# 128-row score matmuls, inverse root of the query and key norms on GpSimd, a split residual: a hybrid decoder layer on one core

## The chip, the cores and the metric

One core of a Trainium2 chip (trn2). The time is device microseconds for one execution of the whole program; the number given for a kernel is the median of its runs. Engines are named as in the profile: PE is TensorE's matmuls and PEld its weight loads, DVE is VectorE, ACT is ScalarE, POOL is GpSimd, SP is the queue that issues most of the DMAs.

## The reference

One step of a decoder layer with 1024 prompt tokens and 8 sequences of 4 sample tokens, model width 1024. Attention (4 heads, each a pair of 64-wide query and key halves) and an RG-LRU recurrence share the input and the output projection; a gated FFN with a width-3 convolution follows. What the change touches is the prompt's attention and the sum that follows it:

```python
q = partial_rope(rmsnorm(q.reshape(bsz, t_len, ATT_HEADS, 2, QK_SUB_DIM), p['g_q']), pos)
k = partial_rope(rmsnorm(k.reshape(bsz, t_len, ATT_HEADS, 2, QK_SUB_DIM), p['g_k']), pos)
...
s = jnp.einsum('bqhcd,bkhcd->bhcqk', q, k) * (QK_SUB_DIM ** -0.5)
s = jnp.where(mask, s, jnp.finfo(F32).min)
p = jax.nn.softmax(s, axis=-1)
p_diff = p[:, :, 0] - lam * p[:, :, 1]
o = jnp.einsum('bhqk,bkhd->bqhd', p_diff, v)
...
m = jnp.concatenate([attn_out, lru_out], axis=-1) @ p['w_out']
x = x + gt1 * m
```

## The kernel before

Nearly every product is made of three fp32r matmuls, high by high, low by high and high by low part of the two operands (`mm3`, L153 to L157). The program has five stages: norm, modulation and LRU with its projections (to about 190 us of the profiled execution), the value projection (190 to 235), prompt attention (245 to 517), output projection with sample attention and the second norm (517 to 690), and the FFN (690 to the end). The order of instructions on each engine is set by a scheduler that simulates the program on a timeline; each engine then runs its own queue in that order, and a transfer waits in SP's queue behind what stands ahead of it.

Prompt attention runs over 16 groups g = head h by pair of 128-row query blocks pr. Each group has these parts, interleaved with those of its neighbours:

- `qk_mm` projects queries and keys three groups ahead. `qk_norm` calls `sums` (ACT copies and squares, DVE reduces to 8 sums of squares per row) and `normed`: DVE L660 and the eleven instructions of `rsqrt_dve` (L136 to L142) give the inverse root on 128x8 elements, then POOL multiplies (L662, L666) and applies rope (L673 to L676, tile rp).
- `qk_T` transposes on PE and splits queries and keys into parts. QA holds for each c (0 and 1) 128 rows: the high part of one half of the query in the 64 rows of that c, and its low part in the other 64. KA holds the high part of the key twice, so that one 128-row matmul gives high by high and low by high. KL holds the low part of the key, the two halves c one above the other.
- `score(g, x, c)` for query block x of the pair and softmax c: per 256 keys one 128-row matmul of QA and KA (L744) and one matmul on the 64 rows `me` of QA and KL (L745); then a mask matmul (L746), the row maximum on DVE (L750) and the exponential with its row sum on ACT (L752). Its result lies in one of two PSUM banks.
- `combine` (L755 to L764) subtracts the two softmaxes, unnormalised, and writes the first sum times a constant into le, one DVE instruction per block (L764). `pv_T` transposes the result, `pv` multiplies by the values; its output goes through tile oT to DRAM.

The residual x2 (8 blocks m of 128 rows by 1056 columns) is allocated in `output`, after attention's pools are closed, and loaded there in four DMAs by `x2_load` (L1153 and L1156), the first for blocks 0 to 3 and columns 0 to 383. `accumulate` (L1080) adds the output projection to it; the first such sums (L1084) free the PSUM banks that sample attention then takes. In the LRU stage `softplus` works on 128x4 elements (7 DVE instructions, one of ACT, 19 of POOL); its input `lru_lambda` and its work tile sp_e lie in the pool lp.

Of the kernel before, what the change touches and what calls it, by code (L numbers as in the profile page):

```python
# [6 lines left out]
F32 = mybir.dt.float32  # L7
# [137 lines left out]
class Build:  # L145
# [56 lines left out]
    def front(self):  # L202
# [158 lines left out]
        lcs = self.load(lp, "state_lru_conv", [128, 4, NS, 3])  # L361
        lamb = self.load(lp, "lru_lambda", [128, 4])
        wgh = ada.tile([128, 2, 4, 128], F32R, name="wgh")
        wgl = ada.tile([128, 2, 4, 128], F32R, name="wgl")
        lco = lp.tile([128, 4, 27], F32, name="lco")
        lho = lp.tile([128, 4, 9], F32, name="lho")
# [177 lines left out]
        b = proj(3)  # L544
        evac(3, b)
        W.split_to(7)
        ada_next()
# [39 lines left out]
        self.pages = []  # L587
        vpp = pool("v", side="right")
        vp = vpp.__enter__()
        vh = [vp.tile([128, 8, 256], F32R, name=f"vh{b}") for b in range(2)]  # L590
        vl = [vp.tile([128, 8, 256], F32R, name=f"vl{b}") for b in range(2)]

# [36 lines left out]
        lpp.__exit__(None, None, None)  # L629
        SP.dma_start(a["lru_conv_o"], lco)  # L630
        SP.dma_start(a["lru_h_o"], lho)
# [12 lines left out]
        G.tensor_copy(mkb, mk)  # L644
        g64 = "p x (g d) -> p (x g) d"

        def sums(b, X, n, st):

            S.activation(st, b, AF.Copy)
            sq = stage("qk_sq")[:n, :X]  # L650
            S.activation(sq, b, AF.Square)
            ms = p.tile([128, 3, 8], F32, name="qk_ms", tag="qk_ms", bufs=2)
            ms = tuple(ms[:n, j, :4 * X] for j in range(3))
            V.tensor_reduce(ms[0], sq.rearrange(g64, d=64), axis=AX.X, op=ALU.add)
            return ms

        def normed(s, i0, X, n, st):

            ms, y, t = s
# [35 lines left out]
        def qk_T(g):  # L695
# [38 lines left out]
        def score(g, x, c):  # L734
            h, pr = divmod(g, 4)
            n = (2 * pr + x + 1) * 128
            b = sbank("s_ps")
            me = slice(64 * c, 64 * c + 64)
# [10 lines left out]
            l = EX[g, x, "l"]  # L749
            V.tensor_reduce(l[:, c:c + 1], b[:, :n], axis=AX.X, op=ALU.max, negate=True)  # L750
            e = EX[g, x, c] = p.tile([128, 1024], F32, name="p_e", tag=f"p_e{c}", bufs=4 if c == 0 else 2)
            S.activation(e[:, :n], b[:, :n], AF.Exp, bias=l[:, c:c + 1], accum_out=l[:, 2 + c:3 + c])  # L752

        def combine(g, x):


            h, pr = divmod(g, 4)
            i = 2 * pr + x
            n = (i + 1) * 128
            l, p0, p1 = EX.pop((g, x, "l")), EX.pop((g, x, 0)), EX.pop((g, x, 1))  # L760
            V.reciprocal(l[:, 3:4], l[:, 3:4])
            V.scalar_tensor_tensor(l[:, 3:4], l[:, 2:3], lam, l[:, 3:4], op0=ALU.mult, op1=ALU.mult)
# [18 lines left out]
        def pv(g, b):  # L781
# [35 lines left out]
        for g in range(NG):  # L817
# [81 lines left out]
        app.__exit__(None, None, None)  # L899
        vpp.__exit__(None, None, None)  # L900
        self.psb = psp

# [169 lines left out]
    def output(self):  # L1072
        a, V, S, G, PE, SP, W = self.a, self.V, self.S, self.G, self.PE, self.SP, self.W
        pool, act_at = self.pool, self.act_at
        xpp = pool("x2", side="right")
        x2 = xpp.__enter__().tile([128, NK, T], F32, name="x2")
        steps = Steps()
        env = {}

        def accumulate(b, m, i, gt, pl):  # L1080

            t0, tw = TC[i]
            w = min(tw, SEQ - t0)
            V.scalar_tensor_tensor(x2[:, m, t0:t0 + w], b[:, :w], gt[:, m, 0:1], x2[:, m, t0:t0 + w], op0=ALU.mult, op1=ALU.add)  # L1084
            if tw > w:
                t = pl.tile([128, SAMP], F32, name="acc_s", tag="acc_s", bufs=2)
                V.tensor_tensor(t.rearrange("p (s q) -> p s q", s=NS), b[:, w:tw].rearrange("p (s q) -> p s q", s=NS),
                                gt[:, m, 1:, None].to_broadcast([128, NS, DT]), op=ALU.mult)
                V.tensor_tensor(x2[:, m, SEQ:], t, x2[:, m, SEQ:], op=ALU.add)

        def norm2(i, env, acc):
# [15 lines left out]
            if tw > w:  # L1107
                ts = p.tile([128, NK, SAMP], F32, name="u2s", tag=tags[0], bufs=2)
                V.tensor_tensor(ts, x2[:, :, SEQ:], bc[:, None, w:tw].to_broadcast([128, NK, SAMP]), op=ALU.mult)
            ut = None  # L1110
            for k in range(NK + 1):
# [9 lines left out]
                V.scalar_tensor_tensor(t[:, :w], x2[:, k, t0:t0 + w], A[:, k, 0:1], bc[:, :w],  # L1121
                                       op0=ALU.mult, op1=ALU.mult)
# [11 lines left out]
        def squares(i, mg, p, tags, acc):  # L1134
            t0, tw = TC[i]
            for m in range(4 * mg, 4 * mg + 4):
                if acc is None:
                    acc = p.tile([128, 384], F32, name="n2_acc", tag=tags[0], bufs=2)
                    S.activation(acc[:, :tw], x2[:, m, t0:t0 + tw], AF.Square)
                else:  # L1140
                    q = p.tile([128, 384], F32, name="n2_sq", tag=tags[1], bufs=tags[2])
                    S.activation(q[:, :tw], x2[:, m, t0:t0 + tw], AF.Square)
                    (V if mg or i == 2 else G).tensor_tensor(acc[:, :tw], acc[:, :tw], q[:, :tw], op=ALU.add)
# [8 lines left out]

        def x2_load(m, n, t0, tw):  # L1153
            SP.dma_start(x2[:, m:m + n, t0:t0 + tw], a["xT"][m:m + n, :, t0:t0 + tw].rearrange("m p t -> p m t"))

        x2_load(0, 4, 0, 384)  # L1156
        for m in range(4):
# [6 lines left out]
        with pool("ps_c", space=PSUM) as pp:  # L1164
# [74 lines left out]

            V.tensor_copy(x2[:1, 4:, 0:1], gsubT[:1, None].to_broadcast([1, 4, 1]))  # L1240
            V.tensor_copy(x2[:1, :, 384:385], gsubT[:1, None].to_broadcast([1, NK, 1]))
# [29 lines left out]
        with pool("ffn") as p, pool("ps_d", space=PSUM) as pp:  # L1271
# [130 lines left out]
            def down(cs, last):  # L1402
# [4 lines left out]
                while todo:  # L1407
# [9 lines left out]
                    for b, (m, i) in zip(bs, batch):  # L1417
# [7 lines left out]
                        if last:  # L1425
                            SP.dma_start(a["yT"][m][:, t0:t0 + tw], x2[:, m, t0:t0 + tw])
                W.split_to(self.ffn_unit["d", cs[-1]] + 3)
# [11 lines left out]
            SP.dma_start(a["ffn_conv_o"], fo)  # L1439
        xpp.__exit__(None, None, None)  # L1440
        self.sqp.__exit__(None, None, None)
# [131 lines left out]
```

## Time and profile before

| | |
|---|---|
| runs | 1434.02, 1430.48, 1433.25 us; median 1433.25 |
| profiled execution | 1431.46 us |
| its span, first to last instruction | 1429.6 us |
| PE / PEld / DVE / ACT / POOL busy, share of the span | 97% / 91% / 57% / 39% / 30% |
| mean granted clock of PE, share of full speed | 0.978 |
| attention, 245 to 520 us: PE / PEld / DVE / ACT / POOL busy us of 275 | 268.0 / 224.9 / 184.7 / 146.3 / 91.5 |

A busy time says how long an engine had an instruction in work; PE's matmuls overlap, so how dense they are is seen from their starts, not from the busy share. PEld overlaps PE where the load of the next weights runs beside the matmul before. The granted clock is the share of TensorE's full speed that the chip let it run at: 1.00 is 2.4 GHz, 0.50 is 1.2 GHz.

### The profile page before, as it was taken

What the parts mean: (1) busy time and instruction counts of PE and PEld (TensorE: products, weight loads), DVE (VectorE), ACT (ScalarE), POOL (GpSimd) and SP (SyncE); (2) the same over time, 40 slices, a digit from 0 to 9 for tenths busy, and PEclk for the clock granted to TensorE, in tenths of its full rate; (3) what the DMA queues carried; (4) which work ended last, traced back from release to release, by engine and by line L of the source; (5) the groups of instructions that cost most, each with busy time, mean ns of one, the idle gap of its engine ahead of it and who ended that gap; (6) DMA issues with size and microseconds to landing.
All of it is one profiled execution on the core that took longest, in us unless ns stands there. A gap on an engine that the chain in (4) does not pass through costs nothing.

```text
span 1429.6 us, 23840 instructions
## 1 busy us (share of the span) xinstructions
PE 1380.3 (97%) x9520; PEld 1302.9 (91%) x9520; DVE 810.8 (57%) x1700; ACT 553.5 (39%) x981; POOL 427.3 (30%) x504
## 2 busy tenths in 40 slices
PE   3998999999999989999999999999999999999998
PEld 3898999788878777789999999999999999999998
DVE  5759534876667436578764545353545353635356
ACT  4366623554545532326723232314141414142411
POOL 1162114433334022413633232314141414142320
PEclk8999999998999899999999999999999999999999
DMA  8625351101011287502111010102020202020203
GB/s 337 253 91 182 144 186 56 50 16 45 20 42 58 70 299 245 187 29 72 45 45 60 30 60 31 60 30 60 30 70 20 75 16 75 15 74 17 73 16 133
DMA packets 51936, 121.99 MB, mean 85 GB/s; under 512 B 8274, under 2 KB 25554, under 8 KB 48754
## 3 DMA queue, kind: packets, MB, share of 16 engines
q1 hardware_dynamic: 46914, 115.73, 24.1%
q10 hardware_dynamic: 4912, 4.74, 1.0%
q8 instruction: 75, 1.23, 0.4%
q14 instruction: 35, 0.29, 0.1%
HBM read 106.51 MB, written 13.94 MB: 84 GB/s over the span
## 4 chain that ended last, share of the span: by engine, by line
PE 89%; DVE 6%; ACT 2%; DMA 2%; issue 1%; POOL 0%; SPq 0%; DVEq 0%; ACTq 0%; POOLq 0%
PE up L155 12%; PE up L156 12%; PE up L157 12%; PE dn L157 6%; PE dn L156 6%; PE dn L155 6%; PE s_ps L745 3%; PE qk_ps L155 3%; PE qk_ps L156 3%; PE qk_ps L157 3%; PE s_ps L744 2%; PE wo_ps L155 2%; PE wo_ps L157 2%; PE wo_ps L156 1%; PE qk_pt L774 1%
## 5 line engine op out<-in xcount | busy, mean ns | idle before, releaser
L60 POOL TENSOR_TENSOR w_lo<-w_raw,w_hi 128x1024 fp32r<-128x1024 f32 x90 | 223.7, 2494 | 592.4 <-ACT w_hi L59 500.9
L155 PE MATMUL up<-act_h,w_hi 128*128 128x384 f32 (+1 forms) x1056 | 341.4, 324 | 1.9 <-ACT act_h L1129 1.9
L157 PE MATMUL up<-act_h,w_lo 128*128 128x384 f32 (+1 forms) x1056 | 340.2, 323 | 0.8 <-DVE w_lo L60 0.8
L156 PE MATMUL up<-act_l,w_hi 128*128 128x384 f32 (+1 forms) x1056 | 340.8, 323 | 0.0
L1084 DVE SCALAR_TENSOR_TENSOR x<-dn,modT,x 128x384 f32<-128x384 f32 (+1 forms) x264 | 149.6, 570 | 167.9 <-PE dn L157 167.7
L1306 DVE SCALAR_TENSOR_TENSOR fy<-fx,conv_ffn_w,fy 128x1072 f32<-128x1072 f32 (+2 forms) x92 | 137.9, 1500 | 173.2 <-ACT fy L1304 171.9
L155 PEld LDWEIGHTS up<-act_h,w_hi 128*128 128x128 f32 x1056 | 197.9, 188 | 2.4 <-ACT act_h L1129 2.2
L157 PEld LDWEIGHTS up<-act_h,w_lo 128*128 128x128 f32 x1056 | 198.3, 188 | 1.1 <-DVE w_lo L60 1.1
L59 ACT ACTIVATE w_hi<-w_raw 128x1024 fp32r<-128x1024 f32 x94 | 98.0, 1057 | 261.7 <-PE dn L156 151.3
L156 PEld LDWEIGHTS up<-act_l,w_hi 128*128 128x128 f32 x1056 | 198.3, 188 | 0.0
L157 PE MATMUL dn<-hh,w_lo 128*128 128x384 f32 (+1 forms) x528 | 170.5, 323 | 0.0
L156 PE MATMUL dn<-hl,w_hi 128*128 128x384 f32 (+1 forms) x528 | 170.5, 323 | 0.0
L155 PE MATMUL dn<-hh,w_hi 128*128 128x384 f32 (+1 forms) x528 | 169.7, 321 | 0.0
L155 PEld LDWEIGHTS dn<-hh,w_hi 128*128 128x128 f32 x528 | 99.2, 188 | 0.0
L157 PEld LDWEIGHTS dn<-hh,w_lo 128*128 128x128 f32 x528 | 99.1, 188 | 0.0
L156 PEld LDWEIGHTS dn<-hl,w_hi 128*128 128x128 f32 x528 | 99.1, 188 | 0.0
L155 PE MATMUL qk_ps<-w_hi,act_h 128*128 128x256 f32 (+1 forms) x288 | 85.9, 298 | 0.0
L157 PE MATMUL qk_ps<-w_hi,act_l 128*128 128x256 f32 (+1 forms) x288 | 84.1, 292 | 0.0
L156 PE MATMUL qk_ps<-w_lo,act_h 128*128 128x256 f32 (+1 forms) x288 | 84.1, 292 | 0.0
L750 DVE TENSOR_REDUCE ls<-s_ps 128x1 f32<-128x128 f32 (+7 forms) x64 | 48.1, 755 | 54.1 <-PE s_ps L746 53.8
L155 PE MATMUL wo_ps<-act_h,w_hi 128*128 128x384 f32 (+1 forms) x192 | 62.7, 338 | 2.8 <-ACT p_e L752 1.1
L156 PE MATMUL wo_ps<-act_l,w_hi 128*128 128x384 f32 (+1 forms) x192 | 62.4, 326 | 0.0
(323 smaller groups left out, 2653.4 us busy)
## 6 DMA issues: line engine op xcount, KB each, us to landing
w_ada<-w_ada SPq DMA_DIRECT2D x24, 1024.0 KB, 6.3
w_raw<-w_up SPq DMA_DIRECT2D x44, 512.0 KB, 3.6
w_raw<-w_down SPq DMA_DIRECT2D x22, 512.0 KB, 3.5
w_raw<-w_in SPq DMA_DIRECT2D x20, 512.0 KB, 3.7
page<-cache_v SPq DMA_DIRECT2D x32, 256.0 KB, 5.0
xT<-xT SPq DMA_DIRECT2D x8, 528.0 KB, 7.9
w_raw<-w_out SPq DMA_DIRECT2D x8, 512.0 KB, 3.8
kp<-cache_k SPq DMA_DIRECT2D x16, 256.0 KB, 4.7
```

Of the source, the lines that this page charges most:

```text
L59: self.nc.scalar.activation(hi, self.raw[i], AF.Copy)
L60: (eng or self.nc.gpsimd).tensor_tensor(lo, self.raw[i], hi.bitcast(F32), op=ALU.subtract)
L155: self.PE.matmul(out, lh, rh, start=first, stop=False)
L156: self.PE.matmul(out, lh, rl, start=False, stop=False)
L157: self.PE.matmul(out, ll, rh, start=False, stop=last)
L744: PE.matmul(o, q, KA[4 * h + kp][:, c, :w], start=True, stop=False, skip_group_check=True)
L745: PE.matmul(o, q[me], KL[4 * h + kp][me, :w], start=False, stop=not last, skip_group_check=True)
L750: V.tensor_reduce(l[:, c:c + 1], b[:, :n], axis=AX.X, op=ALU.max, negate=True)
L774: PE.transpose(t[:, o:o + 128], PD[g, x][:, (2 * b + kk) * 128:(2 * b + kk + 1) * 128], ident)
L1084: V.scalar_tensor_tensor(x2[:, m, t0:t0 + w], b[:, :w], gt[:, m, 0:1], x2[:, m, t0:t0 + w], op0=ALU.mult, op1=ALU.add)
L1306: post.append(lambda c0=c0, c1=c1, j=j: V.scalar_tensor_tensor(y[:, c0:c1], x[:, c0 + j:c1 + j], fw[:, ci, j:j + 1], y[:, c0:c1], op0=ALU. ...
```

## The change

1. **128-row scores.** Two new tiles QZ (128 rows, taken in turn by even and odd groups) are set to zero once on POOL. In every group POOL copies the 64 rows of each c of QA into QZ; the other 64 rows stay zero. The second matmul of each 256 keys takes QZ and all 128 rows of KL in place of 64 rows of each.
2. **Inverse root on POOL.** L660 and the eleven instructions of `rsqrt_dve` in `normed` become two POOL instructions, a multiply-add and a power of -0.5.
3. **First sum in place.** The exponential of c = 0 writes its row sum straight into le; the 32 DVE instructions of L764 become one at the end of attention.
4. **Residual in two tiles.** x2a (blocks 0 to 3) takes the place of the values of heads 0 and 1 in the same buffer and is loaded by one DMA in group 9. x2b (blocks 4 to 7) is allocated and loaded after attention, in two DMAs.
5. **Buffers.** The exponentials have one buffer for each c, x (and parity of pr for c = 0), smaller than before; oT shares rp's single buffer; `softplus`'s input, its work tile and the tile lco lie in the pool ada, and the scheduler then places `softplus` earlier, among the DVE instructions that make the first high and low parts of the normed input.

```diff
-        e = lp.tile([128, 4, 4], F32, name="sp_e")
+        e = ada.tile([128, 4, 4], F32, name="sp_e")
...
+        self.x2p = pool("v", side="right")
+        x2p = self.x2p.__enter__()
+        vpp = pool("stage", side="right")
         vp = vpp.__enter__()
...
+        v01 = x2p.tile([128, 4 * T], F32R, name="v0", tag="v", bufs=1)[:, :4096]
...
+        nhalf = p.tile([128, 8], F32, name="nhalf")
+        G.memset(nhalf, -0.5)
...
-            V.tensor_scalar(ms, ms, 1.0 / 64, EPS, op0=ALU.mult, op1=ALU.add)
-            rsqrt_dve(V, y, t, ms)
+            G.tensor_scalar(y, ms, 1.0 / 64, EPS, op0=ALU.mult, op1=ALU.add)
+            G.tensor_tensor(y, y, nhalf[:n, :4 * X], op=ALU.pow)
...
+        QZ = [p.tile([128, 2, 256], F32R, name=f"QZ{i}") for i in range(2)]
+        for t in QZ:
+            G.memset(t.bitcast(F32), 0.0)
...
+                G.tensor_copy(QZ[g % 2][me[c], c], qa[me[c], c])
...
-            q = QA[g][:, c, x * 128:(x + 1) * 128]
+            q, qz = (t[:, c, x * 128:(x + 1) * 128] for t in (QA[g], QZ[g % 2]))
...
                 PE.matmul(o, q, KA[4 * h + kp][:, c, :w], start=True, stop=False, skip_group_check=True)
-                PE.matmul(o, q[me], KL[4 * h + kp][me, :w], start=False, stop=not last, skip_group_check=True)
+                PE.matmul(o, qz, KL[4 * h + kp][:, :w], start=False, stop=not last, skip_group_check=True)
...
-            e = EX[g, x, c] = p.tile([128, 1024], F32, name="p_e", tag=f"p_e{c}", bufs=4 if c == 0 else 2)
-            S.activation(e[:, :n], b[:, :n], AF.Exp, bias=l[:, c:c + 1], accum_out=l[:, 2 + c:3 + c])
+            e = EX[g, x, c] = p.tile([128, ((6, 8)[pr % 2 or c] - 1 + x) * 128], F32, name="p_e",
+                                     tag=f"p_e{c}{x}{'' if c else pr % 2}", bufs=1)
+            S.activation(e[:, :n], b[:, :n], AF.Exp, bias=l[:, c:c + 1], accum_out=l[:, 2:3] if c else l0)
...
-            V.scalar_tensor_tensor(le[:, i, h:h + 1], l[:, 2:3], 128 * EPS, l[:, 2:3], op0=ALU.mult, op1=ALU.mult)
...
-                ot = p.tile([128, 256], F32, name="oT", tag="oT", bufs=1)
+                ot = p.tile([128, 256], F32, name="oT", tag="rp", bufs=1)
...
+            if g == 9:
+                self.x2 = [x2p.tile([128, 4, T], F32, name="x2a", tag="v", bufs=1)]
+                SP.dma_start(self.x2[0], a["xT"][0:4].rearrange("m p t -> p m t"))
...
+        V.scalar_tensor_tensor(le, le, 128 * EPS, le, op0=ALU.mult, op1=ALU.mult)
...
-        x2_load(0, 4, 0, 384)
+        x2_load(0, 384)
...
-            x2_load(4, 4, 0, 384)
-            x2_load(0, 4, 384, T - 384)
-            x2_load(4, 4, 384, T - 384)
+            x2_load(384, T - 384)
```

PE's queue at the scores of a group with two times 256 keys. Before (each row is an instruction: line, operation, out<-in, shape of the output):

```order
L156 MATMUL qk_ps<-w_lo,act_h_66 128x256
L157 MATMUL qk_ps<-w_hi,act_l_67 128x256
L744 MATMUL s_ps<-KA,QA 128x256
L745 MATMUL s_ps<-KL,QA 128x256
L744 MATMUL s_ps<-KA,QA 128x256
L745 MATMUL s_ps<-KL,QA 128x256
L746 LDWEIGHTS idb
L746 MATMUL s_ps<-mkb,idb 128x128
L744 MATMUL s_ps<-KA,QA 128x256
```

With the change, at the same place:

```order
L156 MATMUL qk_ps<-w_lo,act_h_66 128x256
L157 MATMUL qk_ps<-w_hi,act_l_67 128x256
L755 MATMUL s_ps<-KA,QA 128x256
L756 MATMUL s_ps<-KL,QZ_2240 128x256
L755 MATMUL s_ps<-KA,QA 128x256
L756 MATMUL s_ps<-KL,QZ_2240 128x256
L757 LDWEIGHTS idb
L757 MATMUL s_ps<-mkb,idb 128x128
L155 MATMUL pv_ps<-pTh,v_1693 128x256
```

The low-part matmul has QZ for its weights; the count of matmuls is the same, and six value matmuls have moved between this score and the next.

POOL's queue around a norm, before:

```order
L662 TENSOR_TENSOR qk_st<-qk_st,qk_ms 128x512
L666 TENSOR_TENSOR qk_st<-qk_st,g_qk 128x256 x2
L673 TENSOR_TENSOR rp<-qk_st,rope 128x128
L674 TENSOR_TENSOR rp<-qk_st,rope 128x8x8
L675 TENSOR_TENSOR rp<-qk_st,rope 128x8x8
L676 TENSOR_TENSOR qk_st<-rp 128x8x16
L60 TENSOR_TENSOR w_lo<-w_raw,w_hi 128x1024 x2
```

With the change, from the end of one norm into the next:

```order
L682 TENSOR_TENSOR qk_st<-rp 128x8x16
L718 COPY QZ_2239<-QA 64x256 x2
L666 TENSOR_SCALAR qk_ms<-qk_ms 128x8
L667 TENSOR_TENSOR qk_ms<-qk_ms,nhalf 128x8
L718 COPY QZ_2240<-QA 64x256 x2
L668 TENSOR_TENSOR qk_st<-qk_st,qk_ms 128x512
L60 TENSOR_TENSOR w_lo<-w_raw,w_hi 128x1024
L672 TENSOR_TENSOR qk_st<-qk_st,g_qk 128x256 x2
L60 TENSOR_TENSOR w_lo<-w_raw,w_hi 128x1024
```

The norm has two instructions more at its head (L666, L667), and the pairs of copies into QZ stand in the same queue, here one pair behind the end of a norm and one in the middle of the next; w_lo is the low part of a block of weights.

SP's queue with the change, in attention and after it:

```order
L703 DMA k_o<-qk_st 128x2x128 x3
L858 DMA x2a<-xT 128x4x1056
L50 DMA w_raw<-w_out 128x1024 x2
...
L50 DMA w_raw<-w_out 128x1024
L1174 DMA x2b<-xT 128x4x384
L1170 DMA gsubT<-g_sub_col 128x1
...
L931 DMA cat<-scr_l 128x384 x2
L1174 DMA x2b<-xT 128x4x672
```

The load of blocks 0 to 3 now stands between stores of keys in the middle of attention; before, four loads of x stood in the places of the two x2b rows (one in the first, three in the second).

## Rows read from the trace of the kernel before

**Rows 1.** The page: busy time by engine; the chain that ended last.

```profile
PE 1380.3 (97%) x9520; PEld 1302.9 (91%) x9520; DVE 810.8 (57%) x1700; ACT 553.5 (39%) x981; POOL 427.3 (30%) x504
...
PE 89%; DVE 6%; ACT 2%; DMA 2%; issue 1%; POOL 0%; SPq 0%; DVEq 0%; ACTq 0%; POOLq 0%
```

**Rows 2.** Windows: stretch, its length, busy by engine, granted clock, DMA share, GB/s.

```profile
245.00:520.00 275.00, 267.98 (x1652) 224.90 (x1652) 184.65 (x526) 146.29 (x338) 91.52 (x140) 0.94 0.18 57
300.00:510.00 210.00, 207.38 (x1267) 175.07 (x1266) 138.69 (x397) 114.26 (x260) 70.40 (x110) 0.92 0.19 59
515.00:520.00 5.00, 1.54 (x9) 1.22 (x7) 0.64 (x2) 0.00 (x0) 0.00 (x0) 1.00 0.80 212
350.00:355.00 5.00, 5.00 (x23) 4.77 (x24) 3.66 (x12) 1.91 (x5) 1.17 (x5) 0.50 0.11 30
```

**Rows 3.** Timeline, PE and PEld, 336.6 to 338.5: start, duration, engine, line, shape.

```profile
336.59 0.36 PE L744 MATMUL s_ps<-KA,QA 128*128 128x256 f32 x1
...
337.51 0.18 PEld L745 LDWEIGHTS s_ps<-KL,QA 64*128 64x128 f32 x1
337.51 0.38 PE L745 MATMUL s_ps<-KL,QA 64*128 64x256 f32 x1
...
338.46 0.23 PE L746 MATMUL s_ps<-mkb,idb 128*128 128x128 bf16 x1
```

**Rows 4.** Timeline, PE: a run of 128-row matmuls, 339.17 to 343.96.

```profile
339.17 0.28 PE L155 MATMUL qk_ps<-w_hi,act_h 128*128 128x256 f32 x1
...
343.44 0.28 PE L155 MATMUL pv_ps<-pTh,vh 128*128 128x256 f32 x1
...
343.85 0.27 PE L156 MATMUL pv_ps<-pTl,vh 128*128 128x128 f32 x1
343.96 0.28 PE L157 MATMUL pv_ps<-pTh,vl 128*128 128x128 f32 x1
```

**Rows 5.** Timeline, PE: a score's last 128 keys.

```profile
347.32 0.33 PE L744 MATMUL s_ps<-KA,QA 128*128 128x128 f32 x1
...
347.83 0.23 PE L746 MATMUL s_ps<-mkb,idb 128*128 128x128 bf16 x1
```

**Rows 6.** Tile s_ps: duration ns min/median/max, first and last start, shapes.

```profile
L744 PE MATMUL s_ps<-KA,QA x160: 219/364/581, 245.0 to 497.0; 128*128 128x256 f32 x128, 128*128 128x128 f32 x32
...
L745 PE MATMUL s_ps<-KL,QA x160: 322/381/579, 245.2 to 497.3; 64*128 64x256 f32 x128, 64*128 64x128 f32 x32
```

**Rows 7.** DVE, 245 to 520: tile qk_ms in all; its L654 (ns); L764 in all.

```profile
245.00:520.00 275.00, 52.73 (x227) 0.94 0.18 57
...
L654 DVE TENSOR_REDUCE qk_ms<-qk_sq x17: 399/674/682, 249.7 to 459.0; 128x8 f32<-128x512 f32 x13, 32x4 f32<-32x256 f32 x4
...
245.00:520.00 275.00, 6.12 (x32) 0.94 0.18 57
```

**Rows 8.** Groups of POOL, 240 to 517: busy us, mean ns, idle before.

```profile
L60 POOL TENSOR_TENSOR w_lo<-w_raw,w_hi 128x1024 fp32r<-128x1024 f32 x9 | 21.6, 2416 | 70.4 <-ACT w_hi L59 37.3 <-ACT pTh L777 33.2
L666 POOL TENSOR_TENSOR qk_st<-qk_st,g_qk 128x256 f32<-128x256 f32 x30 | 21.4, 734 | 1.2
...
L962 POOL COPY qblk<-qsT 64x32 f32<-64x32 f32 x8 | 3.0, 376 | 0.4
```

**Rows 9.** Timeline of softplus, DVE and POOL.

```profile
76.95 1.96 DVE L488 TENSOR_SCALAR sp_e<-lru_lambda 128x4 f32<-128x4 f32 x1 [0.34 <-DMA lru_lambda<-lru_lambda]
...
81.12 0.16 DVE L495 TENSOR_TENSOR sp_e<-sp_e 128x4 f32<-128x4 f32 x1
...
82.69 1.17 POOL L498 TENSOR_TENSOR sp_e<-sp_e 128x4 f32<-128x4 f32 x1
...
90.19 0.20 POOL L498 TENSOR_TENSOR sp_e<-sp_e 128x4 f32<-128x4 f32 x1
```

**Rows 10.** PE's waits, whole span: us in total, times, longest.

```profile
PE pg L155 <- DVE modT L277: 4.9, 1, 4.9
PE sa_pn L992 <- DVE x L1084: 4.1, 1, 4.1
```

More of the change, by code (lines that the diff above doesn't have):

```diff
@@ L361, in front @@
         lcs = self.load(lp, "state_lru_conv", [128, 4, NS, 3])
-        lamb = self.load(lp, "lru_lambda", [128, 4])
+        lamb = self.load(ada, "lru_lambda", [128, 4])
         wgh = ada.tile([128, 2, 4, 128], F32R, name="wgh")
         wgl = ada.tile([128, 2, 4, 128], F32R, name="wgl")
-        lco = lp.tile([128, 4, 27], F32, name="lco")
+        lco = ada.tile([128, 4, 27], F32, name="lco")
         lho = lp.tile([128, 4, 9], F32, name="lho")
@@ L545, in front @@
         evac(3, b)
+        SP.dma_start(a["lru_conv_o"], lco)
         W.split_to(7)
@@ L587, in front @@
         self.pages = []
-        vpp = pool("v", side="right")
+        self.x2p = pool("v", side="right")
+        x2p = self.x2p.__enter__()
+        vpp = pool("stage", side="right")
         vp = vpp.__enter__()
-        vh = [vp.tile([128, 8, 256], F32R, name=f"vh{b}") for b in range(2)]
-        vl = [vp.tile([128, 8, 256], F32R, name=f"vl{b}") for b in range(2)]
+        v01 = x2p.tile([128, 4 * T], F32R, name="v0", tag="v", bufs=1)[:, :4096]
+        v01 = [v01.rearrange("p (z t c) -> p z t c", z=2, t=8), vp.tile([128, 2, 8, 256], F32R, name="v1")]
+        vh, vl = ([t[:, z] for t in v01] for z in range(2))
         def stage(name):
@@ L651, in sums @@
             S.activation(sq, b, AF.Square)
-            ms = p.tile([128, 3, 8], F32, name="qk_ms", tag="qk_ms", bufs=2)
-            ms = tuple(ms[:n, j, :4 * X] for j in range(3))
+            ms = p.tile([128, 2, 8], F32, name="qk_ms", tag="qk_ms", bufs=2)
+            ms = tuple(ms[:n, j, :4 * X] for j in range(2))
             V.tensor_reduce(ms[0], sq.rearrange(g64, d=64), axis=AX.X, op=ALU.add)
@@ L706, in qk_T @@
                 S.activation(qa[me[c], c], b[me[c], 0], AF.Copy, scale=0.125)
+            for c in range(2):
+                G.tensor_copy(QZ[g % 2][me[c], c], qa[me[c], c])
             for c in range(2):
@@ L900, in front @@
         vpp.__exit__(None, None, None)
+        self.x2bp = pool("x2b", side="right")
+        self.x2.append(self.x2bp.__enter__().tile([128, 4, T], F32, name="x2b"))
         self.psb = psp
@@ L1074, in output, with x2 @@
         pool, act_at = self.pool, self.act_at
-        xpp = pool("x2", side="right")
-        x2 = xpp.__enter__().tile([128, NK, T], F32, name="x2")
+        def x2(m, c0, c1):
+            return self.x2[m > 3][:, m - 4 * (m > 3), c0:c1]
         steps = Steps()
@@ L1088, in accumulate @@
                                 gt[:, m, 1:, None].to_broadcast([128, NS, DT]), op=ALU.mult)
[L1089 removed]
+                V.tensor_tensor(x2(m, SEQ, T), t, x2(m, SEQ, T), op=ALU.add)
         def norm2(i, env, acc):
@@ L1108, in norm2 @@
                 ts = p.tile([128, NK, SAMP], F32, name="u2s", tag=tags[0], bufs=2)
-                V.tensor_tensor(ts, x2[:, :, SEQ:], bc[:, None, w:tw].to_broadcast([128, NK, SAMP]), op=ALU.mult)
+                for z, (m0, m1) in enumerate(((0, 4), (4, NK))):
+                    V.tensor_tensor(ts[:, m0:m1], self.x2[z][:, :, SEQ:],
+                                    bc[:, None, w:tw].to_broadcast([128, m1 - m0, SAMP]), op=ALU.mult)
             ut = None
@@ L1151, in output, with x2_load @@
         V.tensor_scalar(gsubT, gsubT, 1.0 - LAM0, None, op0=ALU.mult)
-        def x2_load(m, n, t0, tw):
-            SP.dma_start(x2[:, m:m + n, t0:t0 + tw], a["xT"][m:m + n, :, t0:t0 + tw].rearrange("m p t -> p m t"))
-        x2_load(0, 4, 0, 384)
+        def x2_load(t0, tw):
+            SP.dma_start(self.x2[1][:, :, t0:t0 + tw], a["xT"][4:, :, t0:t0 + tw].rearrange("m p t -> p m t"))
+        x2_load(0, 384)
         for m in range(4):
@@ L1238, in output @@
             self.lru_cat_stage(1, stage)
-            V.tensor_copy(x2[:1, 4:, 0:1], gsubT[:1, None].to_broadcast([1, 4, 1]))
-            V.tensor_copy(x2[:1, :, 384:385], gsubT[:1, None].to_broadcast([1, NK, 1]))
-            x2_load(4, 4, 0, 384)
-            x2_load(0, 4, 384, T - 384)
-            x2_load(4, 4, 384, T - 384)
+            for t0 in (384,):
+                V.tensor_copy(self.x2[1][:1, :, t0:t0 + 1], gsubT[:1, None].to_broadcast([1, 4, 1]))
+            x2_load(384, T - 384)
             for i in range(3):
@@ L1425, in down @@
                         if last:
-                            SP.dma_start(a["yT"][m][:, t0:t0 + tw], x2[:, m, t0:t0 + tw])
+                            SP.dma_start(a["yT"][m][:, t0:t0 + tw], x2(m, t0, t0 + tw))
                 W.split_to(self.ffn_unit["d", cs[-1]] + 3)
@@ L1439, in output @@
             SP.dma_start(a["ffn_conv_o"], fo)
-        xpp.__exit__(None, None, None)
+        self.x2bp.__exit__(None, None, None)
+        self.x2p.__exit__(None, None, None)
         self.sqp.__exit__(None, None, None)
```

18 lines of the change are left out of this document (8 added, 10 removed).

## The prediction

> **What bounds the kernel now.** I read the page first: PE is busy 97% of the span and 89% of the chain that ended last lies on it [rows 1], so time can only come from making PE's own work denser or from its few waits. The windows show where it is not dense: of the 275 us of attention PE counts as busy in all but 7.0, 3.5 of them in 515 to 520, yet its granted clock is only 0.94 there and 0.92 from 300 to 510 [rows 2]. The other engines have room: DVE 184.7, ACT 146.3, POOL 91.5 us.
>
> The timeline then shows what "busy" hides. Where 128-row and 64-row score matmuls alternate, six start in 338.46 - 336.59 = 1.87 us, 0.312 each; the weight load of a 64-row matmul begins at the same hundredth as its matmul (337.51) and takes 0.18 [rows 3]. So loading stands ahead of the multiplying. In a run of matmuls of the same size that all have 128 rows, and new weights each time too, 36 start in 343.44 - 339.17 = 4.27 us, 0.119 each [rows 4]: there the loads are hidden. For 128 columns it is (347.83 - 347.32) / 2 = 0.255 in scores [rows 5] against 0.11 in a 128-row run [rows 4].
>
> **The change part by part.** All sums are against the profiled execution, 1431.46 us, 1.8 below the median of 1433.25.
>
> *128-row scores.* There are 128 pairs of score matmuls with 256 columns and 32 with 128 [rows 6]. If they go at the pitch of the 128-row runs: 256 x (0.312 - 0.119) = 49.4 and 64 x (0.255 - 0.11) = 9.3, together **-58.7 us**. It is on the path, since PE is. The other end, nothing, is the first rival.
>
> *The clock.* From 300 to 510 the clock lost is 210 x 0.08 = 17 us; one stretch at half clock (0.50) is 350 to 355 [rows 2], right behind scores. It falls where PE computes sparsely, which scores at 0.312 are. With denser scores most should come back, but 60 us less also means that other waits stand closer together. Bounds 8 (half) and 17; I take **-14**.
>
> *Copies into QZ.* 32 copies of 64x256 on POOL. The nearest rows are 0.376 for 64x32 and 0.734 for a product of 128x256 [rows 8]: 12 to 23 us in all, taken as 0.55 each, 17.6. POOL has the room, so their work costs nothing; where they stand in its queue is another matter, below.
>
> *Inverse root.* From DVE go, in the stage, all of qk_ms's 52.7 but L654's 13 x 0.67 + 4 x 0.40 = 10.4, so 42.3, and of L764 6.1 [rows 7]: DVE falls from 184.7 to 136. For POOL come two instructions for each of 18 norms. No row has a power. Small instructions of the same kind took 0.20 to 1.17 us on POOL [rows 9], 36 x that is 7 to 42; I take 0.5, 18 us. POOL then stands at 91.5 + 17.6 + 18 = 127, at most 157. After the first two terms PE needs 275 - 59 - 14 = 202. PE covers both engines, so the part costs nothing and gains nothing by itself. ACT, which the change leaves at 146, is the next behind PE.
>
> *New waits.* Every score now also waits for POOL, whose queue is in order: the copies stand behind norms (1.05 + 2 x 0.73 us and rope) and sometimes behind w_lo, 2.4 us [rows 8]. POOL's rope waits in turn for oT's store, and ACT's oT for rope, since they share a buffer; and a score still holds one of two PSUM banks through maximum and exponential. With the PE work squeezed, DVE (136), ACT (146) and POOL (127) all stand at two thirds of PE's 202, so queues in order will meet more often than before, when PE lost 3.5 us in the first 270. Below: 5. Above: 16 groups each lose one w_lo, 16 x 2.4 = 38, say 40. I take **+17**, about one microsecond for each group, nearer the lower end since the scheduler keeps three groups of projections ahead of the scores.
>
> *Residual.* Sample attention's first matmul waited 4.1 us for the sums on x [rows 10], and 515 to 520 holds 1.54 us of PE's work [rows 2]. x2a is loaded in group 9 of 16, long before. The 3.5 idle us of that window go, with what the clock loses behind the stall; bounds 3 and 4.5, **-3.5**. What is late next is x2b's blocks, needed one round of sums later.
>
> *First sum in place, buffers, softplus.* The first is in the DVE count above. `softplus` moves to among the instructions that make the first operands of the projections: seven DVE instructions at 0.16 to 1.96 [rows 9], 1.1 to 14 us, of which 0.2 each is the likely size since the 1.96 stands out. Out of its old place it also frees DVE there, ahead of the point where PE waited 4.9 for it [rows 10]. Bounds -1 and +4; **+1**.
>
> Sum: -58.7 - 14 + 17 - 3.5 + 1 = -58.2; 1431.5 - 58.2 + 1.8 = **1375 us** as a median. All bounds at their good end give -58.7 - 17 + 5 - 4.5 - 1 = -76, 1357; all at the bad end -58.7 - 8 + 40 - 3 + 4 = -26, 1407.
>
> **The rivals.**
>
> *Zero rows buy nothing.* The added rows multiply zeros, and 0.18 us of load could be exposed by something other than the row count, such as the reuse of a bank by successive matmuls. For it: every score pair also accumulates in one bank. Against: the 36 projections accumulate in one bank just so, at 0.119 [rows 4]. Then 0.312 stays and only the residual's 3.5 less a few us of new waits is left: about 1432, no change. The Trainium skill's page "TensorE: Matmul & The Clock Gate", section "LDWEIGHTS (loading the stationary operand)", speaks for this rival: a load takes its time from the columns of the weights, and 32 rows take as long as 128. By that rule alone the term would be 0 in place of -58.7. The trace agrees on the load's own length (0.18 at 64 rows) but not on what the rule would make of the pitch. Chance 0.03.
>
> *Another queue sets the pace.* PE gets denser but waits: a score's bank is held while DVE and ACT take maximum and exponential, and the copy into QZ or oT's wait for rope delays them. For it: three engines at two thirds of PE, all in order. Against: before, PE waited 3.5 us in 270. The stage would then take about 240 us in place of 275, 1433 - 35 = 1398, anywhere from 1392 to 1410. Chance 0.17.
>
> *The power is slow, and the kernel slower.* The one operation without a row is the power on POOL. If each took 10 us, POOL would have 91.5 + 17.6 + 18 x 10.5 = 298 us of work in the stage, which then becomes POOL's: 298 - 275 = +23, about 1455. POOL overtakes PE's new 216 from (216 - 109) / 18 = 5.9 us for each norm's pair, and makes the kernel slower than before from (275 - 109) / 18 = 9.2. Against: no row of POOL on tiny operands is over 1.2 us. Chance 0.03.
>
> *The change does not do what it says.* The order shows QZ as the weights of each low-part matmul and nothing on 64 rows left in the scores; I give this no chance of its own.
>
> **How the numbers follow.** Forecast 0.77, the slower queue 0.17, zero rows 0.03, slow power 0.03. The range runs from near the good bounds, 1355, to where most of the second rival lies, 1404; it leaves out the two small cases, what of the second rival lies above, and little below. A measurement of this kernel tells about 0.3% from no change, 4.3 us; the forecast and the slower queue are both far beyond: faster 0.94, within 0.3% 0.03, slower 0.03.
>
> **What would show it.** In the profile after: score matmuls at starts 0.12 apart, with their loads beside the matmul before; a granted clock near 1.00 through 300 to 510; attention some 215 to 220 us long; POOL 120 to 130 us in it, a power at well under 2 us; more PE idle time ended by QZ, QA or the exponential than the 3.5 us before; no wait of sample attention for x. It is wrong if scores still start 0.3 apart, if a power takes over 5 us, or if PE's idle time in attention is above 40 us.

## The result, and the profile after

The changed kernel takes 1380.64 us (median of 4 runs, 1378.86 to 1383.26) against 1431.87 us before (4 runs): a ratio of 0.9644, 95% interval 0.962 to 0.9667. The forecast was 1375 us, with a range of 1355 to 1404. The profiled execution has a span of 1378.9 us, 50.7 less than before.

The page of the changed kernel, busy time by engine and the chain that ended last [rows 1]:

```profile
PE 1322.3 (96%) x9520; PEld 1278.8 (93%) x9520; DVE 782.0 (57%) x1429; ACT 551.6 (40%) x981; POOL 481.3 (35%) x579
...
PE 82%; DVE 7%; ACT 5%; DMA 2%; issue 2%; POOL 1%; SPq 0%; ACTq 0%; DVEq 0%; POOLq 0%
```

PE still bounds the kernel, but its share of the chain is 7 points lower. Where the 50.7 us went is seen from three marks in the timeline of PE: the first score, the end of the last value matmul, and the first matmul of the FFN. The end of the value projection is a fourth mark, used further below.

| stage, us of the span | before | after | difference |
|---|---|---|---|
| start to the first score | 244.97 | 246.93 | +2.0 |
| first score to the end of the last value matmul (attention) | 269.26 | 220.24 | -49.0 |
| from there to the first matmul of the FFN (output) | 139.76 | 135.97 | -3.8 |
| FFN | 775.60 | 775.72 | +0.1 |

The window of attention in the changed kernel (columns as in [rows 2]: stretch, length, busy of PE, PEld, DVE, ACT, POOL, clock, DMA share, GB/s):

```profile
247.00:467.00 220.00, 206.56 (x1640) 198.38 (x1641) 154.53 (x287) 144.37 (x337) 136.40 (x205) 0.98 0.24 77
```

Almost the same count of matmuls as before takes 220 us in place of 269, the granted clock is 0.98 in place of 0.94, and PE idles 13.4 us in place of 3.6. From first score to last value matmul, stretches at half clock add up to 34.1 us in the profile of the kernel before and to 10.2 in this one. What such a stretch costs shows in the projections of the kernel before at 352 us, which start 0.21 apart, against 0.12 at full clock [rows 4]:

```profile
352.10 0.41 PE L157 MATMUL qk_ps<-w_hi,act_l 128*128 128x256 f32 x1
352.31 0.41 PE L155 MATMUL qk_ps<-w_hi,act_h 128*128 128x256 f32 x1
```

The timeline of PE and PEld in a score of the changed kernel shows what became denser [rows 3, 5]:

```profile
386.46 0.36 PE L755 MATMUL s_ps<-KA,QA 128*128 128x256 f32 x1
...
386.66 0.27 PE L756 MATMUL s_ps<-KL,QZ 128*128 128x256 f32 x1
...
386.77 0.28 PE L755 MATMUL s_ps<-KA,QA 128*128 128x256 f32 x1
386.77 0.19 PEld L756 LDWEIGHTS s_ps<-KL,QZ 128*128 128x128 f32 x1
386.89 0.28 PE L756 MATMUL s_ps<-KL,QZ 128*128 128x256 f32 x1
...
387.31 0.27 PE L756 MATMUL s_ps<-KL,QZ 128*128 128x128 f32 x1
387.42 0.23 PE L757 MATMUL s_ps<-mkb,idb 128*128 128x128 bf16 x1
```

The load for the matmul at 386.89 starts at 386.77, beside the matmul before it; scores of 256 columns start 0.12 us apart, as the projections do [rows 4], and the last one, of 128 columns, takes 0.11 to the mask. The score's first matmul, behind a transpose, starts its successor 0.20 later.

The groups of POOL in attention (columns: instruction, shapes, count, busy us, mean ns, idle before) show the two additions, and PE's waits (us, times, longest) what now ends its idle time:

```profile
L667 POOL TENSOR_TENSOR qk_ms<-qk_ms,nhalf 128x8 f32<-128x8 f32 x14 | 23.3, 1666 | 0.8
...
L718 POOL CAST QZ<-QA 64x256 fp32r<-64x256 f32 x30 | 13.8, 459 | 15.5 <-ACT QA L716 10.8 <-PE qk_ps L157 3.5
```

```profile
PE s_ps L755 <- DVE QA L723: 4.6, 4, 2.0
PE s_ps L755 <- ACT p_e L764: 4.5, 5, 2.8
```

A power on 128x8 takes 1.67 us on POOL, over three times the 0.5 that the forecast took for each of the norm's two instructions, a copy 0.46. Scores wait for the query's low part from DVE and for a PSUM bank that an exponential still reads, 9.1 us together; no wait of sample attention for x is left [rows 10].

### The profile page after: what moved, and what is told of

The parts are those of the page before. It is cut to its first block, busy times and chain, and to the rows that moved or that the text cites. A ratio compares the mean times of both kernels' runs of the same rounds, so it can differ in the third digit from the quotient of the medians.

```text
span 1378.9 us, 23666 instructions
## 1 busy us (share of the span) xinstructions
PE 1322.3 (96%) x9520; PEld 1278.8 (93%) x9520; DVE 782.0 (57%) x1429; ACT 551.6 (40%) x981; POOL 481.3 (35%) x579
## 4 chain that ended last, share of the span: by engine, by line
PE 82%; DVE 7%; ACT 5%; DMA 2%; issue 2%; POOL 1%; SPq 0%; ACTq 0%; DVEq 0%; POOLq 0%
PE up L155 12%; PE up L156 12%; PE up L157 12%; PE dn L157 6%; PE dn L156 6%; PE dn L155 6%; PE qk_ps L155 2%; PE wo_ps L155 2%; PE qk_ps L156 2%; PE qk_ps L157 2%; PE wo_ps L157 2%; PE wo_ps L156 2%; PE v_ps L157 1%; PE v_ps L156 1%; PE s_ps L755 1%
## 5 line engine op out<-in xcount | busy, mean ns | idle before, releaser
L1102 DVE SCALAR_TENSOR_TENSOR x2a<-dn,modT,x2a 128x384 f32<-128x384 f32 (+1 forms) x132 | 74.3, 567 | 98.5 <-PE dn L157 98.5
L1102 DVE SCALAR_TENSOR_TENSOR x2b<-dn,modT,x2b 128x384 f32<-128x384 f32 (+1 forms) x132 | 75.4, 573 | 69.4 <-PE dn L157 69.2
```

Source lines behind the costliest of these rows:

```text
L1102: V.scalar_tensor_tensor(x2(m, t0, t0 + w), b[:, :w], gt[:, m, 0:1], x2(m, t0, t0 + w), op0=ALU.mult, op1=ALU.add)
```

## The experiments

For each run the table gives the ratio to before with its interval (runs of the kernel before on the same chip), and from its profile the stages and PE's time in attention: the time from each score matmul's start to the next matmul's, idle taken out, summed over the 320 score matmuls; all other matmuls likewise; and idle.

| run | ratio (95%) | attention | scores | other | idle | output |
|---|---|---|---|---|---|---|
| before | 1 | 269.3 | 94.0 | 171.7 | 3.6 | 139.8 |
| after | 0.9644 (0.962 to 0.9667) | 220.2 | 41.5 | 165.3 | 13.4 | 136.0 |
| e1_scores_only | 0.9759 (0.9729 to 0.979) | 235.9 | 44.3 | 170.4 | 21.2 | 139.7 |
| e2_64row_back | 1.0043 (1.002 to 1.0066) | 274.8 | 95.5 | 172.9 | 6.4 | 134.6 |
| e3_grouped_64row | 0.9723 (0.9693 to 0.9753) | 229.2 | 56.8 | 163.6 | 8.8 | 139.9 |
| e5_root_on_dve | 0.9784 (0.9753 to 0.9816) | 242.1 | 45.4 | 170.7 | 26.0 | 134.3 |
| e6_x_late | 0.9668 (0.964 to 0.9696) | 221.6 | 41.5 | 166.4 | 13.7 | 141.8 |
| e8_grouped_rest | 0.972 (0.9693 to 0.9747) | 228.8 | 56.9 | 163.7 | 8.2 | 134.1 |
| e14_rest_old_buffers | one run, 1432.88 us | 272.9 | 92.8 | 175.2 | 4.9 | 134.1 |
| e4_softplus_late | 0.9634 (0.9605 to 0.9662) | 216.5 | 40.5 | 162.3 | 13.7 | 134.9 |
| after_same_chip | 0.9651 (0.9628 to 0.9674) | 220.7 | 41.3 | 165.8 | 13.6 | 134.5 |
| e4b_softplus_late | 0.9657 (0.9633 to 0.968) | 220.0 | 41.4 | 164.2 | 14.4 | 134.4 |
| e15_zero_padded_keys | 0.9607 (0.9582 to 0.9632) | 217.4 | 39.3 | 165.5 | 12.6 | 134.2 |

### The 128-row scores, alone and taken back

e1_scores_only is the kernel before with the 128-row scores, and with the smaller buffers of the exponentials, without which QZ has no room:

```diff
+                G.tensor_copy(QZ[g % 2][me[c], c], qa[me[c], c])
...
-                PE.matmul(o, q[me], KL[4 * h + kp][me, :w], start=False, stop=not last, skip_group_check=True)
+                PE.matmul(o, qz, KL[4 * h + kp][:, :w], start=False, stop=not last, skip_group_check=True)
```

> The kernel before with the 128-row scores alone (QZ and its copies on POOL, and the smaller buffers of the exponentials that make room for it); inverse root on DVE, residual, oT and softplus stay as before. Theory (the exposed weight loads at every change between 64 and 128 rows were the cost): score matmuls start 0.12 to 0.14 us apart, the stage from the first score to the last value matmul falls from 269 to about 222 us, the kernel to about 1385 us (1378 to 1395), although DVE keeps its 185 us in the stage. Rival (the gain came from DVE's relief and the other parts): the stage falls by at most 15 us, 1415 or more; in between, near 1400, DVE at 185 of 222 us would be the next bound.

The scores fell from 94.0 to 44.3 us, nearly as far as in the changed kernel, yet attention only to 235.9 and the kernel to 1394.79 us. The kernel's time is just inside the theory's 1378 to 1395, but attention is 14 us over its 222, near the case in which DVE bounds next. The difference is idle time, 21.2 us, and a clock of 0.95. The window of attention and two of the waits of PE in it:

```profile
245.00:481.00 236.00, 214.84 (x1642) 204.43 (x1643) 193.55 (x524) 145.16 (x338) 104.44 (x170) 0.95 0.19 62
```

```profile
PE s_ps L748 <- DVE QA L716: 5.1, 5, 1.9
PE pv_ps L156 <- DVE pTl L783: 4.4, 5, 2.5
```

DVE is busy 193.6 of 236 us, and PE waits for what it makes. So the zero rows do what the forecast says on PE, but alone they bring 33 of the 49 us of attention.

e2_64row_back is the changed kernel with these two lines reversed and QZ gone.

> The changed kernel with the 64-row scores of before and without QZ; all else of the change stays. Theory: scores back at 0.31 us apart, half-clock stretches back in attention; only the residual's 4 us stay gained and 2 us lost in the front: about 1430 us (1422 to 1435). Rival (DVE's relief or the new order gave the gain): 1400 or less.

Measured 1433.47 us, ratio 1.0043: the scores are back at 95.5 us, and the rest of the change is worth nothing without the dense scores. It gains 5.1 us in output and loses 5.6 in attention. So the two halves do not add up: the scores alone bring 33 us of attention, the rest alone -5.6, both together 49.0.

### Is it the change of row count, or the 64 rows?

e3_grouped_64row keeps 64 rows and only reorders a score. With it, the start flag of the second pair of keys in a bank comes between the two matmuls of the first pair, and the scores of two and more pairs are not the reference's sums; number, shapes and rows of the matmuls are those of before. (e8_grouped_rest, further below, has the same order with one start flag for each bank, and there the sums are right.)

```diff
                 PE.matmul(o, q, KA[4 * h + kp][:, c, :w], start=True, stop=False, skip_group_check=True)
+            for kp in range(pr + 1):
+                w = min(256, n - kp * 256)
+                o = b[:, kp * 256:kp * 256 + w]
+                last = kp == pr
                 PE.matmul(o, q[me], KL[4 * h + kp][me, :w], start=False, stop=not last, skip_group_check=True)
```

> The kernel before with one edit: within a score all 128-row matmuls first, then all 64-row ones. The changes of row count fall from 320 to 128 (two for each of 64 scores). Theory that each change costs (about 0.16 us each, 52 us in all): 192 changes fewer save about 31 us, about 1401, and 64-row matmuls behind one another start 0.12 us apart. Rival that a 64-row matmul always exposes its own load: 64-row matmuls stay 0.3 us apart and only the 96 128-row ones that now follow one another gain, about 16 us, 1416. Rival that the row count has nothing to do with it: 1432.

Measured 1388.87 us, better than any of the three. Its timeline shows a score of four pairs of keys (x4: four matmuls in one row, with the time from the first start to the last end):

```profile
334.70 0.57 PE L744 MATMUL s_ps<-KA,QA 128*128 128x256 f32 x4
...
335.20 0.53 PEld L749 LDWEIGHTS s_ps<-KL,QA 64*128 64x128 f32 x4
335.20 0.68 PE L749 MATMUL s_ps<-KL,QA 64*128 64x256 f32 x4
335.82 0.23 PE L750 MATMUL s_ps<-mkb,idb 128*128 128x128 bf16 x1
```

From the first 128-row matmul to the first 64-row one 0.50 us pass, from there to the mask 0.62: four 64-row matmuls take 0.12 more than four 128-row ones, less than one exposed load of 0.18, where in the order of before each of them exposed one. The four loads are still made (the PEld row). So the cost is in the change of row count, and 64 rows by themselves expose nothing; what holds the load back at a change was not tried. The scores fell by 37.2 us where 31 were expected. With the clock at 0.99 in the window 243 to 473 the other matmuls took 8.1 us less, and idle time was 5.2 more.

The Trainium skill's rule that a load's time does not depend on its rows ("TensorE: Matmul & The Clock Gate", section "LDWEIGHTS (loading the stationary operand)") holds for the load itself: 0.18 with 64 rows [rows 3], 0.19 with 128. That section does not say whether the load is hidden, and that is where the cost lay here.

e8_grouped_rest takes this order into the changed kernel in place of QZ, with the start flag on the first pair of each bank only:

```diff
-                PE.matmul(o, q, KA[4 * h + kp][:, c, :w], start=True, stop=False, skip_group_check=True)
-                PE.matmul(o, qz, KL[4 * h + kp][:, :w], start=False, stop=not last, skip_group_check=True)
+                PE.matmul(o, q, KA[4 * h + kp][:, c, :w], start=kp % 2 == 0, stop=False, skip_group_check=True)
+            for kp in range(pr + 1):
...
+                PE.matmul(o, q[me], KL[4 * h + kp][me, :w], start=False, stop=not last, skip_group_check=True)
```

> The changed kernel with 64-row low-part matmuls grouped behind all 128-row ones of a score, without QZ and its copies; inverse root on POOL and all else of the change stay. Theory (what costs is the change of row count, 128 times here, about 0.12 us each over the 128-row form; POOL loses 14 us of copies, which were not on the path): scores take 56.6 us of PE as in the grouped run on the kernel before, 15 more than with QZ; attention 232 us (226 to 236), ratio to before about 0.971. Rival (the copies behind POOL's queue cost as much as the zero rows save): attention 220 or less, ratio 0.964 or less.

As the theory said: scores 56.9, attention 228.8, ratio 0.972. The 15.4 us that the remaining changes cost are partly given back by 5.2 us less idle and 1.6 less in the other matmuls. PE waits less for QA:

```profile
PE s_ps L751 <- DVE QA L718: 2.2, 2, 1.6
PE s_ps L751 <- ACT p_e L764: 1.5, 3, 1.0
```

That the missing copies are the reason is not shown: e15_zero_padded_keys, further below, has dense scores and no copies, and 12.6 us of idle.

### The inverse root

e5_root_on_dve puts it back on DVE in the changed kernel:

```diff
-            G.tensor_scalar(y, ms, 1.0 / 64, EPS, op0=ALU.mult, op1=ALU.add)
-            G.tensor_tensor(y, y, nhalf[:n, :4 * X], op=ALU.pow)
+            V.tensor_scalar(ms, ms, 1.0 / 64, EPS, op0=ALU.mult, op1=ALU.add)
+            rsqrt_dve(V, y, t, ms)
```

> The changed kernel with the inverse root of the norms back on DVE (twelve instructions on 128x8 for each norm); 128-row scores, copies into QZ and all else stay. The kernel with the scores alone took 236 us for attention, 16 more than the changed one. Theory (DVE at about 185 us in a stage of 220 delays QA, KL and pTl, so its relief is worth those 16): attention about 234 us (228 to 238), the kernel about 1391 us (ratio to before 0.973), PE idle in attention about 20 us. Rival (the 16 came from the first softmax sum's 32 instructions, the shared buffers or the order): attention at most 224 us, ratio 0.966.

Attention took 242.1 us, even more than expected, with 26.0 of idle; the kernel 1399.70 us. Window, and the longest waits of PE in it:

```profile
247.00:489.00 242.00, 215.68 (x1638) 204.75 (x1639) 196.61 (x498) 142.29 (x335) 107.78 (x170) 0.95 0.22 70
```

```profile
PE s_ps L753 <- ACT p_e L762: 8.2, 7, 2.9
PE s_ps L753 <- DVE QA L721: 6.0, 4, 3.0
PE pv_ps L156 <- DVE pTl L787: 4.1, 6, 2.0
```

So with dense scores the inverse root's place is worth 21.9 us of attention (242.1 - 220.2): 12.6 of them are idle time, and 9.3 are matmuls that took longer, with a granted clock of 0.95 in place of 0.98. All three waits hang on DVE, the first through the maximum that the exponential needs: ACT's exponentials wait 51.8 us for the maxima in this stage, 27.5 in the changed kernel. Whether it is DVE's total or the chain of twelve dependent instructions in its queue was not told apart.

### The residual, the buffers, softplus

e6_x_late allocates and loads all of the residual after attention:

```diff
-                SP.dma_start(self.x2[0], a["xT"][0:4].rearrange("m p t -> p m t"))
...
+        self.x2 = [x2bp.tile([128, 4, T], F32, name=n) for n in ("x2a", "x2b")]
...
+            x2_load(1, 0, 384)
+            x2_load(0, 384, T - 384)
+            x2_load(1, 384, T - 384)
```

> The changed kernel with all of the residual allocated and loaded after attention, in four pieces as before. Theory (the early load removes PE's stall of 4 us ahead of sample attention and nothing else): PE waits about 4 us for DVE's x again, 139.8 us from the last value matmul to the first matmul of the FFN in place of 136.0, the kernel 4 us slower than the changed one. Rival (the 3.8 us came from a different order of the sample attention's work): no such wait, 136.

The wait came back, in PE's waits of that run:

```profile
PE sa_pn L1008 <- DVE x2a L1101: 4.6, 1, 4.6
```

The output stage took 141.8 us, 5.8 more than in the changed kernel; the ratio is 0.9668 against 0.9644 and 0.9651. The intervals overlap, but the wait is plain, and the stage took 134.1 to 136.0 us in the nine profiles with x early, 139.7 to 141.8 in the four with x late.

e14_rest_old_buffers is e2_64row_back with the exponentials' and oT's buffers of before:

```diff
+            e = EX[g, x, c] = p.tile([128, 1024], F32, name="p_e", tag=f"p_e{c}", bufs=4 if c == 0 else 2)
...
+                ot = p.tile([128, 256], F32, name="oT", tag="oT", bufs=1)
```

> The changed kernel with the 64-row scores of before and without QZ, which took 274.8 us for attention against 269.3 in the kernel before; here the exponentials have their four and two buffers of before, and oT its own. Theory (the smaller and shared buffers cost those 5.5 us): attention about 269 us. Rival (the power on POOL, 1.67 us for each norm, and the new order cost them): 274 or more.

Attention took 272.9 us, between the two; idle went from 6.4 to 4.9. The buffers cost at most a part of the 5.5 us, and what costs the rest stays open: one profile of each does not part 2 us.

e4_softplus_late, run twice (the second time as e4b_softplus_late, beside the changed kernel), is one line:

```diff
-        lamb = self.load(ada, "lru_lambda", [128, 4])
+        lamb = self.load(lp, "lru_lambda", [128, 4])
```

> The changed kernel with lru_lambda back in the pool lp, which puts softplus back to its place of before. Theory (softplus among the first normed operands costs the front 2 us): the value projection ends at 222.5 in place of 224.5 us of the span, the kernel takes about 1378.6 us. Rival (the 2 us come from elsewhere): no change, 1380.6.

> The changed kernel once more, on the chip of the two runs beside it, so that differences of 2 to 4 us between versions can be read: 0.964 of before.

> The changed kernel with softplus late, beside the changed kernel on the same chip. Theory (softplus among the first operands costs about 2.5 us of the front, as the ends of the value projection in the profiles so far suggest): 2 to 3 us less than the changed kernel. Rival (spread between profiles): within 1 us of it.

In both profiles the value projection ended at 219.9 and 219.5 us, against 224.5 and 224.0 in the two profiles of the changed kernel. Most of that is not softplus. Below are the windows of 20 to 222 us of the kernel before, the changed kernel, e4_softplus_late and e4b_softplus_late; the third number from the end is the granted clock:

```profile
20.00:222.00 202.00, 186.90 (x1813) 177.48 (x1811) 119.81 (x170) 100.64 (x148) 49.30 (x57) 0.94 0.49 178
20.00:222.00 202.00, 186.00 (x1794) 176.90 (x1792) 122.31 (x169) 98.88 (x146) 53.46 (x60) 0.93 0.50 177
20.00:222.00 202.00, 186.34 (x1833) 177.11 (x1831) 120.75 (x170) 102.40 (x150) 51.77 (x62) 0.96 0.50 179
20.00:222.00 202.00, 185.88 (x1836) 176.78 (x1835) 120.53 (x170) 102.22 (x150) 52.10 (x62) 0.97 0.49 179
```

Over the thirteen profiles the end of the value projection goes with this clock: 219.5 us at 0.97, 219.9 at 0.96, 220.9 at 0.95, 222.0 to 224.0 at 0.94 (seven profiles, with softplus in either place), 224.5 to 226.0 at 0.93 (three). Softplus itself shows in PE's waits for the first operands; the largest of them before, then after:

```profile
PE lx L155 <- ACT act_h L304: 1.0, 1, 1.0
```

```profile
PE lx L156 <- DVE act_l L315: 3.2, 2, 2.8
```

All waits of these matmuls (lx) together are 2.8 to 3.3 us in the seven profiles with softplus early and 1.5 to 2.4 in the six with it late. So early softplus costs PE about 1 us; why the clock differs from profile to profile stays open. The medians cannot show 1 us: beside each other they are 1379.41 and 1380.12 us; over all ten runs of each they are 1377.8 and 1380.6, with runs of one kernel 8 to 16 us apart.

### A version without the copies

e15_zero_padded_keys puts the zeros into the keys: DVE writes the low parts straight into fixed tiles, QA serves both matmuls. Softplus is late in it too.

```diff
+        KZ = [p.tile([128, 2, 256], F32R, name=f"KZ{i}") for i in range(5)]
...
-                G.tensor_copy(QZ[g % 2][me[c], c], qa[me[c], c])
...
-                V.tensor_tensor(kl[me[c]], b[me[c], 1], ka[me[c], c].bitcast(F32), op=ALU.subtract)
+                V.tensor_tensor(kl[me[c], c], b[me[c], 1], ka[me[c], c].bitcast(F32), op=ALU.subtract)
...
-                PE.matmul(o, qz, KL[4 * h + kp][:, :w], start=False, stop=not last, skip_group_check=True)
+                PE.matmul(o, q, KL[4 * h + kp][:, c, :w], start=False, stop=not last, skip_group_check=True)
```

> The changed kernel with softplus late and without QZ: the low key parts are written by DVE straight into five fixed tiles KZ whose other 64 rows are zero, for each c apart, so that QA serves both matmuls and POOL copies nothing (to make room, the inverse root works in place with one buffer, and the maxima have three buffers in place of four). Theory (the copies behind POOL's queue cost about 5 us of PE's 13.7 idle in attention, as the grouped run without them had 8.2): idle about 9, attention about 212 us, some 5 us less than the kernel with softplus late, about 0.960 of before. Rival (PE's idle comes from DVE's and ACT's chains alone): attention 216, no change against it.

Its median is 1375.06 us, the lowest of all, and 5.1 below the changed kernel on the same chip. But its neighbour is the kernel with softplus late: it is 4.35 below e4b_softplus_late on the same chip and 2.7 below the ten runs of e4 and e4b together, whose times (1370.5 to 1386.6) overlap its own (1369.7 to 1380.1). Attention took 217.4 us, between the 216.5 (granted clock 1.00) and 220.0 (0.98) of those two. So a gain over softplus late is not shown, and the rival's "no change" stands for attention. The reason that was expected is not borne out: idle fell only to 12.6 us, not to 9. The scores took 39.3 us, against 40.5 and 41.4. What ends PE's idle time now is an exponential first:

```profile
PE s_ps L754 <- ACT p_e L763: 4.0, 6, 1.9
PE s_ps L754 <- DVE QA L722: 2.4, 2, 1.6
```

## Why the prediction was right, and where its steps were not

- **128-row scores, -58.7.** Right in mechanism: pitch 0.12 and 0.11, loads beside the matmul before, and the grouped run shows that the change of row count was the cost. Measured 94.0 to 41.5, -52.5, with some 2 us of recovered clock in it. Mis-sized at both ends: the working took 0.312 and 0.255 for every score matmul, 96.2 us in all, but a score's first matmul follows another 128-row one, and behind a projection its successor starts 0.21 later; and it took 37.5 for after, where a score's first matmul behind transposes or a mask starts its successor 0.20 later (386.46 to 386.66).
- **The clock, -14.** It went from 0.94 to 0.98 in attention. The working took a stretch at half clock as half lost, and nearly all of it as coming back. Set against the same kind of matmul at full clock, the 34.1 us at half clock cost an estimated 15 us before (projections start 0.21 apart in them, less than twice 0.12), and the 10.2 that remain cost 4.6: -10.3. Most of the loss before, some 12 us, lay in matmuls other than scores, which fell by 6.4 in all. The two terms together gave -72.7; PE's matmuls fell by 52.5 + 6.4 = 58.9.
- **Inverse root, nothing by itself.** This is the step that failed. The text had PE, at 202 us, cover the other engines wherever the inverse root stands, which means DVE at its old 185 too; the sentence was "the part costs nothing and gains nothing by itself". With DVE at 196.6 of 242 us, attention is 21.9 us longer. Here an engine at nine tenths of the one that bounds (196.6 us of DVE against 216 of PE), with each waiting for the other, was not covered. The sum came out since the part was there, and since the term for new waits had been made with DVE at 136.
- **DVE 136, POOL 127.** Measured 154.5 and 136.4. The power took 1.67 and the multiply-add beside it 0.22 where 0.5 was taken for each, the copies 0.46 where 0.55. On DVE the 48.4 us taken off were durations that overlap in part with others (before, DVE's instructions in the stage add up to 205 us, and it is busy for 184), and combine's long instruction became slower (below).
- **New waits, +17 (5 to 40).** Idle went from 3.6 to 13.4: +9.8, inside the bounds. The copies, which the working put first, are a small part of it: e15_zero_padded_keys, without them, still has 12.6 us of idle, and PE's longest waits after are for QA's low part from DVE and for the exponential.
- **Residual, -3.5.** The output stage became 3.8 us shorter, and 5.8 longer again when the load was late.
- **Front, +1 (-1 to +4).** +2.0 in the profiles. About 1 us is PE's longer wait for the first operands; the rest goes with a granted clock of 0.93 in place of 0.94 up to the end of the value projection.

The sum of the stages is +2.0 - 49.0 - 3.8 + 0.1 = -50.7 where the steps gave -58.2, 7.5 us too good. Part of this closeness is luck: the two terms of PE's matmuls were 13.8 too good, the new waits 7.2 too bad. The medians differ by 5.6 (1380.6 and 1375), in part since the kernel before now has a median 1.4 lower than the one the forecast was set against. Of the rivals, "zero rows buy nothing" fell with e1, e2 and e3; "the power is slow" was right in direction but at 1.67 us stays far under the 5.9 at which POOL would take over; "another queue sets the pace" is what e1 and e5 show when DVE keeps the inverse root, at 1394.79 and 1399.70 us, on both sides of the 1398 it was priced at.

## What to carry to other kernels

Look at the starts of matmuls, not at a busy share of 97%: where weights of different row counts alternated here, the load was exposed at each change, and both zero rows and an order that groups equal row counts took that back. Before costing an edit on another engine at nothing, divide that engine's work by the bounding engine's new time, not its old one; here the two halves of the change brought 33 and -5.6 us of attention alone and 49.0 together. Compare stages by marks in the traces: with runs of one kernel up to 16 us apart, only the stages showed effects of 2 to 5 us. And read the granted clock of the same stretch beside each mark: up to the end of the value projection, seven profiles with the same code up to there were 4 us apart (222.0 to 226.0), mostly with the clock.

## What the runs showed of the hardware that was not expected

A power by POOL took 1.67 us on 128x8 elements and 1.00 on 32x4, while the multiply-add beside it took 0.22 us on 128x8. And combine's instruction on DVE, the same 32 instructions on the same shapes with two operands in SBUF, went from 27.5 to 31.2 us with POOL busier; the row of before, then of after:

```profile
L763 DVE SCALAR_TENSOR_TENSOR p_e<-p_e,ls 128x128 f32<-128x128 f32 (+7 forms) x32 | 27.5, 859 | 0.3
```

```profile
L775 DVE SCALAR_TENSOR_TENSOR p_e<-p_e,ls 128x128 f32<-128x128 f32 (+7 forms) x32 | 31.2, 975 | 1.1
```

Over the thirteen profiles this instruction's mean follows POOL's busy share of attention: 842 to 859 ns at shares of 0.34 to 0.41, 887 to 896 at 0.43 to 0.45, 924 and 934 at 0.52 and 0.56, 956 to 985 at 0.62 and 0.63. The norm's small instructions on DVE did the same: the same 227 kept DVE busy for 52.7 us before [rows 7], with POOL's share at 0.34, and for 63.8 in e1_scores_only, with POOL's at 0.44:

```profile
245.00:481.00 236.00, 63.83 (x227) 0.95 0.19 62
```

So DVE went from 184.7 to 193.6 us in e1_scores_only though it got no new instruction. The maxima on DVE, which read PSUM, did not change: 48.1 and 47.4 us for the same 64. That POOL is the cause was not tried by itself.
